# A row factor taken out of two norms and put behind the projections, in a two-block transformer kernel on one core

## The chip, the core and the metric

The program runs on one core of one Trainium2 chip, in fp32 data with fp32r matmuls. [...] The metric is the device time of one execution in microseconds.

## The reference

Two blocks follow each other on x of 512 tokens by 1024 columns. Both begin with the same norm and then project its result many times:

```
def rmsnorm(x, g):
    r = lax.rsqrt(jnp.mean(xf * xf, axis=-1, keepdims=True) + EPS)   # one factor per token (row)
    return (xf * r) * g                                              # g: one gain per column

# block 1
h = rmsnorm(x, norm1_g); u, v_a, q, k, v_b = split(h @ w_in)
y_a = chunked_spatial_gating(u, rmsnorm(v_a, ...), w_s, b_s)          # u * z
y_b = rmsnorm(diff_attention(rmsnorm(q), rmsnorm(k), v_b))
gates = sigmoid(h @ w_gate + b_gate)
x = x + (g_a * (y_a @ w_up_a) + g_b * (y_b @ w_up_b)) @ w_out
x = x + hierarchical_moe(rmsnorm(x, norm2_g))                         # 32 experts, top 2
# block 2
xn = _rms(x, norm_gain); proj = xn @ w_in
qkv_a = silu(causal_dwconv(proj[:, :1536], conv_w))                   # 4 taps along the tokens
o_a = gated_delta_rule(l2n(q_a), l2n(k_a), v_a, g, beta);  o_b = stick_breaking(_rms(q_b), _rms(k_b), v_b)
out = x + (gate_a * ((_rms(o_a) * silu(z_a)) @ w_up_a) + gate_b * ((o_b * silu(z_b)) @ w_up_b)) @ w_out
```

r is a scalar per token, so (r·x·g) W = r · ((x·g) W): the factor can be applied ahead of a projection or behind it. In block 2 it has to be applied ahead of the convolution, which mixes tokens.

## The kernel before

Every projection is a call of `dense`: 512 tokens by 512 columns, 1024 deep. SP loads the raw weights in two transfers of 1 MB (raw_q_0 and raw_q_4 for the projection q), ACT casts each quarter (two of the eight 128-row slabs) to a high part in wHL (L58, CAST), and DVE, or POOL for the quarters that `pool_split` names, subtracts to get the low part (L59). For each of eight slabs d and each of four accumulators acc_0 to acc_3 three matmuls of 128x512 are done: high by high, high by low, low by high. `stationary="x"` leaves tokens on the partitions of the accumulator (L89 to L91), `stationary="w"` leaves columns there and tokens along the free side (L93 to L95). The four accumulators come from one pool of four, so the next projection's acc_t can be written only when the evacuation of acc_t, `evac(t)`, has read it; wHL has two buffers and raw two.

The activations are split the same way. `row_rms` squares x on ACT (in block 1 the second half of x on DVE), adds, and finds r by a chain of thirteen small DVE operations (L130, and L40 to L47 in `rsqrt_newton`). `transpose_x` then multiplies all of x by r (L105, eight operations into the tiles xn_h1 or xn_h3), does 32 PE transposes into eight PSUM tiles psT, and splits each into hH (ACT, L52, scaled by the column gain) and hL (DVE, L53). Each slab d of the first projection needs hH and hL of d.

The first projection of block 1 is q (acc_q), then k, v and the rest; of block 2 ak, aq and av (acc_ak, acc_aq, acc_av), which `delta_inputs` evacuates with three convolution taps on DVE (L1025), a copy U and a scaled copy cv on ACT (L1022, L1023), a tanh, and four transposes (psck, pscq, pscv); then qbA, qbB and so on. Ahead of block 2 stands the mixture of experts, whose `combine` adds each pair's result (psc, L854 and L855) to x on DVE (L856). Accumulators psc and acc share a pool.

The order on each engine is set by the tile scheduler from the order of the code, its priorities and the buffers. `issue_after` ties one instruction behind another.

Of the kernel before, what the change touches and what calls it, by code (L numbers as in the profile page):

```python
# [73 lines left out]
def dense(K, xs, W, n0, nk, evac, name, stationary="x", width=512, hook=None):  # L74
# [3 lines left out]
    for k in range(0, nk, 2):  # L78
        wHL = K.wp.tile([P, 2, 2, width], R, name=f"wHL_{name}_{k}", tag="wHL", bufs=K.nwh)
        wH, wL = wHL[:, 0], wHL[:, 1]  # L80
        split_plain(K, wH, wL, raws[k // 4][:, k % 4:k % 4 + 2], nc.gpsimd if k // 2 in K.pool_split else None)
        for kk in range(2):
            d = k + kk
            H, L = xs(d)
            for t in range(4):
                ts = slice(t * P, t * P + P)
                s, e = d == 0, d == nk - 1
                if stationary == "x":
                    nc.tensor.matmul(acc[t][:, :width], H[:, ts], wH[:, kk], start=s, stop=False)  # L89
                    nc.tensor.matmul(acc[t][:, :width], H[:, ts], wL[:, kk], start=False, stop=False)  # L90
                    nc.tensor.matmul(acc[t][:, :width], L[:, ts], wH[:, kk], start=False, stop=e)  # L91
# [117 lines left out]
def first_attention(K, I, hs, filler):  # L209
# [3 lines left out]
    def load_half(hh):  # L213
        tok = {}
        ssq = {}
        for nm, n0 in (("q", 2048), ("k", 3072)):
# [154 lines left out]
def gating(K, I, hs, Vs):  # L371
# [636 lines left out]
def delta_inputs(K, I, hs, W):  # L1008
# [3 lines left out]
    for ti, nm in enumerate(("k", "q", "v")):  # L1012
# [5 lines left out]
        def ev(h, acc, nm=nm, U=U, T=T, col0=col0, ti=ti):  # L1018
# [567 lines left out]
```

## Time and profile before

| what | value |
|---|---|
| median of 3 runs | 1450.3 us (1449.73 to 1450.57) |
| profiled execution | 1450.06 us, of it the span that the trace shows 1448.2 us |
| busy share of the span | PE 95%, DVE 55%, ACT 35%, POOL 6% |
| mean granted clock of TensorE | 0.988 |

A row of the busy table gives, for each engine, the microseconds in which it had an instruction under way and the number of instructions. A row of the timeline gives the start, the time to the end of a run of like instructions, the engine and line, the output and inputs, and in brackets how long the engine had been idle ahead of it and which instruction ended that. A matmul's row lasts from its start to its modelled end and overlaps the next; the distance between starts is the pace.

### The profile page before, as it was taken

What the parts mean: (1) busy time and instruction counts of PE and PEld (TensorE: products, weight loads), DVE (VectorE), ACT (ScalarE), POOL (GpSimd) and SP (SyncE); (2) the same over time, 40 slices, a digit from 0 to 9 for tenths busy, and PEclk for the clock granted to TensorE, in tenths of its full rate; (3) what the DMA queues carried; (4) which work ended last, traced back from release to release, by engine and by line L of the source; (5) the groups of instructions that cost most, each with busy time, mean ns of one, the idle gap of its engine ahead of it and who ended that gap; (6) DMA issues with size and microseconds to landing.
All of it is one profiled execution on the core that took longest, in us unless ns stands there. A gap on an engine that the chain in (4) does not pass through costs nothing.

```text
span 1448.2 us, 18248 instructions
## 1 busy us (share of the span) xinstructions
PE 1371.1 (95%) x7211; PEld 1015.3 (70%) x7211; DVE 795.7 (55%) x1560; ACT 509.2 (35%) x896; POOL 84.0 (6%) x93
## 2 busy tenths in 40 slices
PE   4999999999999997899999997989999999999998
PEld 3777786788888886344444445769889977667886
DVE  5466578683343255455555447587454656563562
ACT  3435436433223231122111214446332237663331
POOL 2000000000000022100000001110000100001000
PEclk9999999999999998899999998999999999999999
DMA  4221221122232478799999832213220000002332
GB/s 152 91 87 31 89 80 64 43 75 88 89 105 98 131 265 301 293 380 369 365 362 364 320 117 88 87 45 103 87 87 2 31 30 29 30 30 67 137 116 88
DMA packets 73756, 196.12 MB, mean 135 GB/s; under 512 B 8658, under 2 KB 10820, under 8 KB 69572
## 3 DMA queue, kind: packets, MB, share of 16 engines
q1 hardware_dynamic: 67460, 184.79, 35.6%
q0 software_dynamic: 3680, 9.44, 1.9%
q8 instruction: 58, 0.95, 0.3%
q10 hardware_dynamic: 2528, 0.69, 0.2%
q14 instruction: 30, 0.25, 0.0%
HBM read 192.81 MB, written 6.29 MB: 137 GB/s over the span
## 4 chain that ended last, share of the span: by engine, by line
PE 83%; DVE 10%; ACT 4%; issue 1%; DMA 1%; POOL 0%; SPq 0%; DVEq 0%; ACTq 0%
PE acc_e L795 8%; PE po L795 4%; PE acc_upbg L93 3%; PE acc_upbg L95 3%; PE acc_upbg L94 3%; PE acc_gbg L95 2%; PE acc_gbg L93 2%; PE acc_gbg L94 2%; PE pss L270 2%; PE psc L854 2%; PE acc_o L89 2%; PE acc_o L90 2%; PE acc_o L91 2%; PE psc L855 1%; PE psG L786 1%
## 5 line engine op out<-in xcount | busy, mean ns | idle before, releaser
L795 PE MATMUL acc_e<-w,S 128*64 128x512 f32 x512 | 121.0, 604 | 0.0
L856 DVE TENSOR_TENSOR x<-x,psc 128x512 f32<-128x512 f32 x128 | 80.3, 680 | 13.5 <-PE psc L855 13.5
L795 PEld LDWEIGHTS acc_e<-w,S 128*64 128x64 f32 x512 | 41.6, 138 | 55.7 <-issue 52.3
L795 PE MATMUL po<-w,th 128*64 128x512 f32 x256 | 58.5, 598 | 8.1 <-DVE th L819 8.1
L59 DVE TENSOR_TENSOR wHL_upbg<-raw_upbg,wHL_upbg 128x1024 fp32r<-128x1024 f32 x24 | 29.3, 1224 | 55.6 <-ACT wHL_upbg L58 55.6
L59 DVE TENSOR_TENSOR wHL_gbg<-raw_gbg,wHL_gbg 128x1024 fp32r<-128x1024 f32 x20 | 24.5, 1224 | 62.3 <-ACT wHL_gbg L58 62.3
L854 PE MATMUL psc<-Y,DT 128*128 128x512 f32 x128 | 57.8, 451 | 0.3
L855 PE MATMUL psc<-Y,DT 128*128 128x512 f32 x128 | 50.6, 395 | 0.0
L91 PE MATMUL acc_o<-wHL_o,mL_bg 128*128 128x512 f32 x128 | 49.9, 390 | 0.0
L90 PE MATMUL acc_o<-wHL_o,mH_bg 128*128 128x512 f32 x128 | 49.8, 389 | 0.0
L95 PE MATMUL acc_gbg<-hH,wHL_gbg 128*128 128x512 f32 x128 | 49.8, 389 | 0.0
L94 PE MATMUL acc_gbg<-hL,wHL_gbg 128*128 128x512 f32 x128 | 49.8, 389 | 0.0
L58 ACT CAST wHL_upbg<-raw_upbg 128x1024 fp32r<-128x1024 f32 x24 | 25.3, 1053 | 69.7 <-PE acc_upbg L95 47.9
L93 PE MATMUL acc_gbg<-hH,wHL_gbg 128*128 128x512 f32 x128 | 49.5, 389 | 0.0
L89 PE MATMUL acc_o<-wHL_o,mH_bg 128*128 128x512 f32 x128 | 49.2, 391 | 0.0
L837 ACT CAST DT<-psD 128x512 fp32r<-128x512 bf16 x16 | 9.4, 587 | 112.0 <-PE psD L834 112.0
L58 ACT CAST wHL_gbg<-raw_gbg 128x1024 fp32r<-128x1024 f32 x20 | 21.1, 1054 | 73.9 <-PE acc_gbg L95 40.5
L795 PEld LDWEIGHTS po<-w,th 128*64 128x64 f32 x256 | 17.4, 136 | 41.9 <-issue 27.0
L59 DVE TENSOR_TENSOR wHL_o<-raw_o,wHL_o 128x1024 fp32r<-128x1024 f32 x16 | 21.3, 1328 | 45.6 <-ACT wHL_o L58 45.6
L854 PEld LDWEIGHTS psc<-Y,DT 128*128 128x128 f32 x128 | 24.1, 188 | 30.8 <-DVE Y L53 12.2
L52 ACT ACTIVATE Y<-po,cslot 128x512 fp32r<-128x512 f32 x32 | 22.0, 688 | 64.0 <-PE po L795 64.0
L787 DVE COPY S<-psG 128x512 f32<-128x512 f32 x16 | 11.1, 692 | 54.5 <-PE psG L786 52.6
(649 smaller groups left out, 3693.7 us busy)
## 6 DMA issues: line engine op xcount, KB each, us to landing
w<-in_w SPq DMA_DIRECT2D x128, 512.0 KB
w<-in_w SPq DMA_DIRECT2D x32, 1024.0 KB
raw_gbg<-in_w_gate SPq DMA_DIRECT2D x8, 1024.0 KB
raw_o<-in_w_out SPq DMA_DIRECT2D x8, 1024.0 KB
raw_upbg<-in_w_up_a SPq DMA_DIRECT2D x6, 1024.0 KB
raw_upbg<-in_w_up_b SPq DMA_DIRECT2D x6, 1024.0 KB
raw_gr<-in_w_in SPq DMA_DIRECT2D x6, 1024.0 KB
raw_q<-in_w_in SPq DMA_DIRECT2D x4, 1024.0 KB
```

Source lines behind the costliest of these rows:

```text
L58: K.last_h = K.nc.scalar.copy(H, src)
L59: return (eng or K.nc.vector).tensor_sub(L, src, H.bitcast(F))
L89: nc.tensor.matmul(acc[t][:, :width], H[:, ts], wH[:, kk], start=s, stop=False)
L90: nc.tensor.matmul(acc[t][:, :width], H[:, ts], wL[:, kk], start=False, stop=False)
L91: nc.tensor.matmul(acc[t][:, :width], L[:, ts], wH[:, kk], start=False, stop=e)
L93: nc.tensor.matmul(acc[t], wH[:, kk, ts], H, start=s, stop=False)
L94: nc.tensor.matmul(acc[t], wH[:, kk, ts], L, start=False, stop=False)
L95: nc.tensor.matmul(acc[t], wL[:, kk, ts], H, start=False, stop=e)
L795: K.mm_last = K.nc.tensor.matmul(out[js], lhsT[:, js], rhs(j), start=start, stop=stop, tile_position=(0, 64 * j))
L854: nc.tensor.matmul(acc, DT[:, t * P:t * P + P], H[:, n], start=True, stop=False)
L855: nc.tensor.matmul(acc, DT[:, t * P:t * P + P], L[:, n], start=False, stop=True)
L856: nc.vector.tensor_add(out[n][:, t], x[n][:, t], acc)
```

## The change

Four things change together. (1) The squares and r are no longer ahead of the transposes: raw x is transposed and split, in two halves of four slabs. The second half is tied behind the first projection's 48th matmul (`second(last)` at k == 4), and the squares and r behind that. Every fourth transposed tile takes another PSUM buffer ("ob"). (2) r is multiplied in the evacuations of all projections that used the normed x. Where tokens are on the partitions, the copy takes r as its scale (ACT) or a scalar multiply is used (DVE). Where tokens are along the free side, `scale_row` spreads r over the partitions with four matmuls, ACT copies it into the tile alibi, and DVE multiplies the accumulator by that tile; this adds a DVE pass to the gates, to z of the gating, to the delta inputs (there in place of an ACT copy) and to za and zb, and moves half the copies of gr from ACT to DVE. (3) The first loads alternate: half of x, half of q's weights, half of x, half of q's weights. (4) `pool_split` is empty for q and ak, so DVE does those two quarters each; the last expert pair's `combine` goes through the first 512 columns of all four token tiles first; and the stores of x2 follow the second half's splits.

```diff
-def dense(K, xs, W, n0, nk, evac, name, stationary="x", width=512, hook=None):
+def dense(K, xs, W, n0, nk, evac, name, stationary="x", width=512, hook=None, second=None):
     for k in range(0, nk, 2):
+        if k == 4 and second is not None:
+            second(last)
...
-                    nc.tensor.matmul(acc[t], wL[:, kk, ts], H, start=False, stop=e)
+                    last = nc.tensor.matmul(acc[t], wL[:, kk, ts], H, start=False, stop=e)
...
-def transpose_x(K, x, rcol, gcol, hs, name):
-    src = [K.t8.tile([P, 4, 512], F, name=f"xn_{name}{n}", tag="t8") for n in range(2)]
-    for half in range(2):
-        for t in range(4):
-            nc.vector.tensor_scalar_mul(src[half][:, t], x[half][:, t], rcol[:, t:t + 1])
+def transpose_x(K, x, gcol, hs, name, half, last=None):
+    with K.tc.issue_after(last.ins) if last is not None else nullcontext():
+        for d in range(4 * half, 4 * half + 4):
+            tag, bufs = ("ob", 1) if d % 4 == 3 else ("b", 3)
+                nc.tensor.transpose(ps[:, t * P:t * P + P], x[half][:, t, (d % 4) * P:(d % 4) * P + P], K.ident)
+            done = split_scaled(K, H, L, ps, gcol[:, d:d + 1])
...
+def scale_row(K, r, name):
+    ps = K.psb.tile([P, 512], F, name=f"psrow_{name}", tag="b", bufs=3)
+    for t in range(4):
+        K.nc.tensor.matmul(ps[:, t * P:t * P + P], r[:, t:t + 1].to_broadcast((P, P)), K.ident, start=True, stop=True)
+    K.nc.scalar.copy(K.alibi, ps)
+    return K.alibi
...   # q and k; v, va, qbA, qbB, kb and vb likewise
-                nc.scalar.copy(T[:, t], acc)
+                nc.scalar.activation(T[:, t], acc, AF.Copy, scale=K.r1[:, t:t + 1])
-                nc.scalar.activation(junk, acc, AF.Square)
+                nc.scalar.activation(junk, T[:, t], AF.Square)
...   # gating
+            nc.vector.tensor_mul(z[:, gg], z[:, gg], K.rrow)
...   # gate units
+        nc.vector.tensor_mul(g[:, t], acc, K.rrow)
-            nc.scalar.activation(g[:, t], acc, AF.Tanh, bias=..., scale=0.5)
+            nc.scalar.activation(g[:, t], g[:, t], AF.Tanh, bias=..., scale=0.5)
...   # first_block
+    def second(last):
+        done = transpose_x(K, xs, K.cc("g1", 0, 8), hs, "h1", 1, last)
+        with prio(K, K.tc.cur_priority + 60), K.tc.issue_after(done.ins), K.tc.issue_after(K.act_split.ins):
+            row_rms(K, xs, K.r1, "n1", True)
...   # combine, last pair
-    for t in ts:
-        for n in range(2):
+    for n, t in ([(n, t) for t in ts for n in range(2)] if out is x else [(n, t) for n in range(2) for t in ts]):
...   # delta_inputs
-            nc.scalar.activation(y, acc, AF.Copy, scale=K.cc("cw", 36 + j0))
-            nc.scalar.copy(U[:, h, 3:515], acc)
+            nc.vector.tensor_mul(U[:, h, 3:515], acc, K.rrow)
+            nc.scalar.activation(y, U[:, h, 3:515], AF.Copy, scale=K.cc("cw", 36 + j0))
-        K.pool_split = (0, 1) if nm == "k" else (1, 3)
+        K.pool_split = () if nm == "k" else (1, 3)
...   # za, zb
-            K.tanh_last = nc.scalar.activation(th, acc, AF.Tanh, scale=0.5)
-            nc.vector.scalar_tensor_tensor(z[:, t], th, 1.0, acc, op0=OP.add, op1=OP.mult)
+            nc.vector.tensor_mul(z[:, t], acc, K.rrow)
+            K.tanh_last = nc.scalar.activation(th, z[:, t], AF.Tanh, scale=0.5)
+            nc.vector.scalar_tensor_tensor(z[:, t], th, 1.0, z[:, t], op0=OP.add, op1=OP.mult)
```

How the order of instructions moves is shown at three places; numbers behind a name tell buffers apart, and x2 or x4 at a row's end is a count.

PE at the start of the program, where q is the first projection; before:

```order
L109 MATMUL psT_h1_0_155<-ident_87,xn_h10_145 128x128 x2
...
L109 MATMUL psT_h1_2_169<-ident_87,xn_h10_145 128x128 x4
L89 MATMUL acc_q0_0_217<-wHL_q0_0_221,hH0_141 128x512
L90 MATMUL acc_q0_0_217<-wHL_q0_0_221,hH0_141 128x512
L109 MATMUL psT_h1_3_176<-ident_87,xn_h10_145 128x128 x4
L91 MATMUL acc_q0_0_217<-wHL_q0_0_221,hL0_142 128x512
L109 MATMUL psT_h1_4_183<-ident_87,xn_h11_146 128x128 x4
```

and of the change, from the first transposes to the second half's (rows of dots stand for rows left out, here matmuls of the first four slabs):

```order
L109 MATMUL psT_h1_0_114<-ident_91,x0_81 128x128 x4
L109 MATMUL psT_h1_1_121<-ident_91,x0_81 128x128 x4
L109 MATMUL psT_h1_2_128<-ident_91,x0_81 128x128 x4
L109 MATMUL psT_h1_3_135<-ident_91,x0_81 128x128 x4
L91 MATMUL acc_q0_0_145<-wHL_q0_0_149,hH0_110 128x512
L91 MATMUL acc_q0_1_146<-wHL_q0_0_149,hH0_110 128x512
L91 MATMUL acc_q0_2_147<-wHL_q0_0_149,hH0_110 128x512
...
L93 MATMUL acc_q0_3_148<-wHL_q0_2_176,hL0_111 128x512
L109 MATMUL psT_h1_4_203<-ident_91,x1_86 128x128 x4
L109 MATMUL psT_h1_5_210<-ident_91,x1_86 128x128 x4
```

The transposes read x itself, and the 20 that stood among the first matmuls are gone: 16 stand ahead of the first matmul, and 16 behind the 48th.

PE where the experts end and block 2 begins (psc15 is the last pair's combine, acc_ak the first projection of block 2); before:

```order
L855 MATMUL psc1530_6665<-Y15_6610,DT15_6571 128x512
L854 MATMUL psc1531_6669<-Y15_6610,DT15_6571 128x512
L855 MATMUL psc1531_6669<-Y15_6610,DT15_6571 128x512
L109 MATMUL psT_h3_0_6726<-ident_87,xn_h30_6716 128x128 x2
L109 MATMUL psT_h3_1_6733<-ident_87,xn_h30_6716 128x128
...
L109 MATMUL psT_h3_2_6740<-ident_87,xn_h30_6716 128x128 x4
L93 MATMUL acc_ak_0_6790<-h3H0_6712,wHL_ak_0_6794 128x512
L93 MATMUL acc_ak_1_6791<-h3H0_6712,wHL_ak_0_6794 128x512
L109 MATMUL psT_h3_3_6747<-ident_87,xn_h30_6716 128x128 x4
L94 MATMUL acc_ak_0_6790<-h3L0_6713,wHL_ak_0_6794 128x512
```

and of the change:

```order
L877 MATMUL psc1501_6677<-Y15_6630,DT15_6591 128x512
L878 MATMUL psc1501_6677<-Y15_6630,DT15_6591 128x512
L109 MATMUL psT_h3_0_6706<-ident_91,x2_0_6659 128x128
L109 MATMUL psT_h3_1_6713<-ident_91,x2_0_6659 128x128
L877 MATMUL psc1511_6681<-Y15_6630,DT15_6591 128x512
...
L877 MATMUL psc1531_6689<-Y15_6630,DT15_6591 128x512
L878 MATMUL psc1531_6689<-Y15_6630,DT15_6591 128x512
...
L109 MATMUL psT_h3_2_6720<-ident_91,x2_0_6659 128x128 x4
L109 MATMUL psT_h3_3_6727<-ident_91,x2_0_6659 128x128 x4
L95 MATMUL acc_ak_0_6744<-h3H0_6702,wHL_ak_0_6748 128x512
L96 MATMUL acc_ak_0_6744<-h3L0_6703,wHL_ak_0_6748 128x512
```

The last pair's matmuls for the first 512 columns come first, and transposes of those columns (x2_0) stand between those for the other 512.

DVE between the projections ak and aq; before:

```order
L59 TENSOR_TENSOR wHL_ak_4_6848<-raw_ak_4_6788,wHL_ak_4_6848 128x1024
L59 TENSOR_TENSOR wHL_ak_6_6875<-raw_ak_4_6788,wHL_ak_6_6875 128x1024
L59 TENSOR_TENSOR wHL_aq_0_6981<-raw_aq_0_6973,wHL_aq_0_6981 128x1024
L1025 SCALAR_TENSOR_TENSOR cvk0_6902<-Uk_6783,ccols_b_346,cvk0_6902 128x512 x2
L1025 SCALAR_TENSOR_TENSOR cvk1_6919<-Uk_6783,ccols_b_346,cvk1_6919 128x512
L1025 SCALAR_TENSOR_TENSOR cvk0_6902<-Uk_6783,ccols_b_346,cvk0_6902 128x512
L1025 SCALAR_TENSOR_TENSOR cvk1_6919<-Uk_6783,ccols_b_346,cvk1_6919 128x512
L1027 SCALAR_TENSOR_TENSOR cvk0_6902<-cthk0_6903,cvk0_6902 128x512
L1025 SCALAR_TENSOR_TENSOR cvk1_6919<-Uk_6783,ccols_b_346,cvk1_6919 128x512
L1037 TENSOR_REDUCE ssqk_6782<-cthk0_6903 128x4
```

and of the change:

```order
L46 TENSOR_TENSOR rt_n3_6843<-rt_n3_6843,rv_n3_6841 128x4
L47 SCALAR_TENSOR_TENSOR r3_6734<-rt_n3_6843,ry_n3_6842 128x4
L1045 TENSOR_TENSOR Uk_6737<-acc_ak_0_6744,alibi_105 128x512
L1045 TENSOR_TENSOR Uk_6737<-acc_ak_1_6745,alibi_105 128x512
...
L1048 SCALAR_TENSOR_TENSOR cvk0_6918<-Uk_6737,ccols_b_336,cvk0_6918 128x512
L1048 SCALAR_TENSOR_TENSOR cvk1_6935<-Uk_6737,ccols_b_336,cvk1_6935 128x512
...
L1048 SCALAR_TENSOR_TENSOR cvk1_6935<-Uk_6737,ccols_b_336,cvk1_6935 128x512
L1045 TENSOR_TENSOR Uk_6737<-acc_ak_3_6747,alibi_105 128x512
L1050 SCALAR_TENSOR_TENSOR cvk0_6918<-cthk0_6919,cvk0_6918 128x512
L1050 SCALAR_TENSOR_TENSOR cvk1_6935<-cthk1_6936,cvk1_6935 128x512
L1060 TENSOR_REDUCE ssqk_6736<-cthk0_6919 128x4
```

The multiplies from acc_ak, which need r3 and its spread in alibi, stand ahead of the taps, and the one of acc_ak_3 behind six of them. On PE 27 matmuls that write acc_aq_0, 1 and 2 now stand ahead of the first that writes acc_aq_3; before, 24 that write acc_aq_0 and 1 stood ahead of the first that writes acc_aq_2.

## Rows read from the trace of the kernel before

**Rows 1.** The page, part 1, and two of its groups: line, engine, operation, count | busy, mean ns.

```profile
PE 1371.1 (95%) x7211; PEld 1015.3 (70%) x7211; DVE 795.7 (55%) x1560; ACT 509.2 (35%) x896; POOL 84.0 (6%) x93
...
L856 DVE TENSOR_TENSOR x<-x,psc 128x512 f32<-128x512 f32 x128 | 80.3, 680 | 13.5 <-PE psc L855 13.5
...
L59 DVE TENSOR_TENSOR wHL_upbg<-raw_upbg,wHL_upbg 128x1024 fp32r<-128x1024 f32 x24 | 29.3, 1224 | 55.6 <-ACT wHL_upbg L58 55.6
```

**Rows 2.** Busy time by stage: stretch, its length, each engine's busy time, granted clock.

```profile
0.00:45.20 45.20, 26.37 (x121) 21.65 (x122) 22.77 (x52) 14.77 (x23) 7.40 (x13) 1.00 0.46 145
45.20:263.00 217.80, 214.43 (x1071) 165.65 (x1070) 142.36 (x365) 100.63 (x219) 1.61 (x2) 1.00 0.22 73
...
877.60:914.10 36.50, 27.73 (x129) 22.94 (x130) 19.50 (x33) 13.55 (x21) 4.63 (x2) 0.86 0.34 116
914.10:985.00 70.90, 61.58 (x307) 49.72 (x306) 55.10 (x85) 37.81 (x63) 10.47 (x7) 0.98 0.17 53
985.00:1160.00 175.00, 174.39 (x1281) 154.50 (x1281) 94.68 (x181) 56.88 (x104) 9.78 (x22) 1.00 0.20 64
```

**Rows 3.** The timeline of the start, three engines: start, duration, operation, idle before.

```profile
4.70 0.63 ACT L128 ACTIVATE junk_n<-x 128x512 f32<-128x512 f32 x1 [1.70 <-DMA x<-in_x]
...
13.13 1.99 ACT L58 CAST wHL_q<-raw_q 128x1024 fp32r<-128x1024 f32 x2 [5.45 <-DMA crows_b<-in_k_norm_g]
...
14.46 2.20 DVE L47 SCALAR_TENSOR_TENSOR r<-rt_n,ry_n 128x4 f32<-128x4 f32 x1
16.70 5.29 DVE L105 TENSOR_SCALAR xn_h<-x,r 128x512 f32<-128x512 f32 x8
...
19.27 3.01 PE L109 MATMUL psT_h<-ident,xn_h 128*128 128x128 f32 x12 [14.29 <-DVE xn_h L105]
21.93 0.78 PE L89 MATMUL acc_q<-wHL_q,hH 128*128 128x512 f32 x1
...
26.84 0.39 PE L90 MATMUL acc_q<-wHL_q,hH 128*128 128x512 f32 x1
...
29.82 0.39 PE L91 MATMUL acc_q<-wHL_q,hL 128*128 128x512 f32 x1
```

**Rows 4.** The timeline around the second block's first norm, VectorE and TensorE.

```profile
869.66 7.85 DVE L856 TENSOR_TENSOR x<-x,psc 128x512 f32<-128x512 f32 x13
...
879.97 2.34 DVE L46 TENSOR_TENSOR rt_n<-rt_n,rv_n 128x4 f32<-128x4 f32 x1
...
885.82 3.26 DVE L105 TENSOR_SCALAR xn_h<-x,r 128x512 f32<-128x512 f32 x8
...
886.37 3.00 PE L109 MATMUL psT_h<-ident,xn_h 128*128 128x128 f32 x12 [10.46 <-DVE xn_h L105]
889.02 1.20 PE L93 MATMUL acc_ak<-h3H,wHL_ak 128*128 128x512 f32 x2
```

**Rows 5.** TensorE's waits from 877 to 990 us: who waited for whom, total, times, longest.

```profile
PE acc_qbA L90 <- DVE wHL_qbA L59: 2.7, 1, 2.7
...
PE psck L1030 <- DVE cvk L1027: 2.0, 2, 1.5
...
PE acc_aq L95 <- POOL wHL_aq L59: 0.5, 1, 0.5
```

**Rows 6.** Busy time of two stretches at the lower clock.

```profile
880.40:890.60 10.20, 4.23 (x17) 3.50 (x18) 9.92 (x19) 2.37 (x4) 4.19 (x2) 0.50 0.62 214
...
972.50:976.00 3.50, 2.92 (x13) 2.92 (x14) 2.40 (x4) 0.58 (x2) 0.00 (x0) 0.51 0.49 137
```

**Rows 7.** Groups by shape, ScalarE, 0 to 263 us.

```profile
L52 ACT ACTIVATE hH<-psT_h,ccols_a 128x512 fp32r<-128x512 f32 x8 | 5.4, 688 | 7.0 <-PE psT_h L109 7.0
...
L221 ACT COPY qtok<-acc_q 128x512 f32<-128x512 f32 x8 | 4.8, 598 | 5.6 <-PE acc_q L91 5.6
```

**Rows 8.** Groups by shape, VectorE, 877.6 to 1448.2 us.

```profile
L1025 DVE SCALAR_TENSOR_TENSOR cvk<-Uk,ccols_b,cvk 128x512 f32<-128x512 f32 x12 | 10.8, 926 | 2.7 <-ACT Uk L1023 2.6
...
L1025 DVE SCALAR_TENSOR_TENSOR cvv<-Uv,ccols_b,cvv 128x512 f32<-128x512 f32 x12 | 8.6, 746 | 0.4 <-ACT Uv L1023 0.4
```

More of the change, by code (lines that the diff above doesn't have):

```diff
@@ L51, in split_scaled @@
 def split_scaled(K, H, L, src, gain):
-    K.nc.scalar.activation(H, src, AF.Copy, scale=gain)
+    K.act_split = K.nc.scalar.activation(H, src, AF.Copy, scale=gain)
     return K.nc.vector.scalar_tensor_tensor(L, src, gain, H.bitcast(F), op0=OP.mult, op1=OP.subtract)
@@ L59, in split_plain, with load_w @@
     return (eng or K.nc.vector).tensor_sub(L, src, H.bitcast(F))
-def load_w(K, W, n0, width, nk, name, hook=None):
-    parts = []
-    for q in range(0, nk, 4):
+def load_w(K, W, n0, width, nk, name, hook=None, qs=None):
+    parts = K.ahead.pop(name, [])
+    for q in range(4 * len(parts), nk, 4) if qs is None else qs:
         raw = K.wp.tile([P, 4, width], F, name=f"raw_{name}_{q}", tag="raw", bufs=K.nraw)
@@ L90, in dense @@
                     nc.tensor.matmul(acc[t][:, :width], H[:, ts], wL[:, kk], start=False, stop=False)
-                    nc.tensor.matmul(acc[t][:, :width], L[:, ts], wH[:, kk], start=False, stop=e)
+                    last = nc.tensor.matmul(acc[t][:, :width], L[:, ts], wH[:, kk], start=False, stop=e)
                 else:
@@ L451, in first_block @@
     xr = I["x"][0].rearrange("(t p) d -> p t d", p=P)
+    K.ahead["q0"] = []
     for half in range(2):
@@ L456, in first_block @@
         xs.append(t)
+        K.ahead["q0"] += load_w(K, I["w_in"][0], 2048, 512, 8, "q0h", qs=(4 * half,))
     consts_early(K, I)
     K.alibi = alibi(K)
-    r = K.sm.tile([P, 4], F, name="r1")
-    row_rms(K, xs, r, "n1", True)
     h = []
@@ L465, in first_block @@
     hs = sel(h)
-    transpose_x(K, xs, r, K.cc("g1", 0, 8), hs, "h1")
+    transpose_x(K, xs, K.cc("g1", 0, 8), hs, "h1", 0)
+    K.r1 = K.sm.tile([P, 4], F, name="r1")
+    def second(last):
+        done = transpose_x(K, xs, K.cc("g1", 0, 8), hs, "h1", 1, last)
+        with prio(K, K.tc.cur_priority + 60), K.tc.issue_after(done.ins), K.tc.issue_after(K.act_split.ins):
+            row_rms(K, xs, K.r1, "n1", True)
+    K.second = second
     yb, Vs = first_attention(K, I, hs, lambda: gate_values(K, I, hs))
+    K.rrow = scale_row(K, K.r1, "n1")
     consts2(K)
@@ L1360, in second_block @@
     W = I["w_in_2"][0]
-    r3 = K.sm.tile([P, 4], F, name="r3")
-    row_rms(K, x2, r3, "n3", big=K.t8.tile([P, 4, 512], F, name="sqjunk", tag="t8"))
-    K.h_after = K.sq_last
-    for n in range(2):
-        nc.sync.dma_start(x2d.rearrange("(t p) d -> p t d", p=P)[:, :, 512 * n:512 * n + 512], x2[n])
     h = []
@@ L1370, in second_block, with second @@
     hs = sel(h)
-    transpose_x(K, x2, r3, K.cc("g3", 0, 8), hs, "h3")
+    transpose_x(K, x2, K.cc("g3", 0, 8), hs, "h3", 0)
+    r3 = K.sm.tile([P, 4], F, name="r3")
+    sqjunk = K.t8.tile([P, 4, 512], F, name="sqjunk", tag="t8")
+    def second(last):
+        done = transpose_x(K, x2, K.cc("g3", 0, 8), hs, "h3", 1, last)
+        with prio(K, K.tc.cur_priority + 60), K.tc.issue_after(done.ins), K.tc.issue_after(K.act_split.ins):
+            row_rms(K, x2, r3, "n3", big=sqjunk)
+            K.rrow = scale_row(K, r3, "n3")
+            for n in range(2):
+                nc.sync.dma_start(x2d.rearrange("(t p) d -> p t d", p=P)[:, :, 512 * n:512 * n + 512], x2[n])
+    K.second = second
     tok, r = delta_inputs(K, I, hs, W)
@@ L1421, in ev @@
         def ev(t, acc):
-            if t % 2:
-                nc.scalar.copy(Z[:, t], acc)
-            else:
-                nc.vector.tensor_copy(Z[:, t], acc)
+            nc.vector.tensor_mul(Z[:, t], acc, K.rrow)
         dense(K, hs, W, n0, 8, ev, nm, stationary="w")
@@ L1516, in body @@
     K.act_mark = K.load_after = K.h_after = None
+    K.ahead = {}
     K.pool_split = ()
```

42 lines of the change are left out of this document (22 added, 20 removed).

## The prediction

> **What bounds the kernel now.** I read the page's busy table first, then busy time by stage, TensorE's waits, and the timelines where it waits. PE is busy 95% of the span, DVE 55%, ACT 35% [rows 1]. So only PE's idle time can be won, and added work on DVE or ACT costs only where PE waits for it. The stages show where: from 45.2 to 263 us PE is busy 214.43 of 217.80 us, and from 985 to 1160 us 174.39 of 175; but in the first 45.20 us only 26.37, from 877.6 to 914.1 us 27.73 of 36.50, and from 914.1 to 985 us 61.58 of 70.90 [rows 2]. The first two of these poor stretches are the two norms that the change takes apart. The third is the delta inputs, to which it adds work.
>
> At the start PE does nothing useful until 19.27 us: its wait of 14.29 us ends on xn_h, the multiply by r [rows 3]. x was there far earlier, since ACT squares its first tile at 4.70. Between lie the squares, r's chain (its last step, usually some 0.16 us, took 2.20 beside POOL's weight split) and eight multiplies of 5.29 us from 16.70 [rows 3]. The same picture stands at block 2: DVE's additions to x run 869.66 + 7.85 = 877.51, and the first transpose comes at 886.37 after 10.46 us of idle PE [rows 4].
>
> **Term A, the start.** Before, the first q matmul stands at 21.93 and q ends at the stage's end, 45.20. After, the transposes need only x's first half. It has landed by about 6.2 us (an estimate: its first part by 4.70, the second one 0.5 MB transfer later). Sixteen transposes at 3.01/12 = 0.25 us each [rows 3] make 4 us when they wait for nothing: about 9.4 with the hand-over to PSUM, and hH of the fourth slab about 10.3, a split being 0.69 us [rows 7]. The weights' first half now comes third in line, about 9.5. Its cast, 1.99/2 = 1.0 us [rows 3], stands behind the four hH on ACT: first matmul at 11.35. From there: 96 matmuls at (29.82 − 26.84)/13 = 0.23 us [rows 3], 21.8 us; 16 warm transposes at an estimated 0.1 (under half the cold price, since they overlap matmuls), 1.6; the first ten or so at the lower clock, twice the price, 1.9; and 0.6 in the middle, where hH4 stands behind a cast on ACT and PE reaches the fifth slab first. Together 25.9, so q ends near 37.2 instead of 45.2: −8.0. r is ready at about 36.4 (four squares on each of ACT and DVE behind the second splits, r's chain, one weight split of 1.22 us [rows 1] in it), so q's evacuations nearly wait for it; k's first matmul may lose 0.2 more. **A = −7.8**, bounds −5 (weights late by 2 us, and r by 1) and −10 (no extra cold time, no stall in the middle).
>
> **Term B, block 2.** The last pair's first 512 columns are done first. Of the 13 additions, 7.85/13 = 0.60 us each [rows 4], the last four then belong to the second half: x's first half is complete at 877.51 − 4 × 0.60 = 875.1. Its transposes mix with the last combine matmuls; hH of the slabs ends at about 876.5, 877.5, 878.5 and 879.2; the cast of ak's weights follows on ACT, so acc_ak starts at about 880.3, not 889.02 [rows 4]. The low parts on DVE wait for the additions and end at 881.8 with the weights' own. Before, ak took 914.1 − 889.02 = 25.1 us with 20 transposes among its matmuls and its first ones at the lower clock [rows 2, 4]; after, 24.0 with 16 transposes and the same clock. ak ends at 904.3 instead of 914.1: **B = −9.8**, bounds −7.5 and −10.5. The lower bound is a stall of 2 us: r3 is ready only at about 904.8, since eight squares, r's chain and a weight split stand behind the second splits.
>
> The clock is the open point of B. It fell to 0.50 from 880.40 to 890.60, after PE had stood still since 886.37 − 10.46 = 875.91 [rows 4], and PE was busy only 4.23 us in that stretch [rows 6]. After, PE stands still from about 877.4 to 880.3, a third as long. If the clock is then full, B gains another 1 us; I keep it low for the first matmuls. [...]
>
> **Term C, the delta inputs.** Three projections, each evacuated in four steps. Removed: ACT's copy U. Added: one DVE multiply per step from PSUM, 12 at 0.60 to 0.68 us by the addition of the same form [rows 1, 4], 7.7 us, beside 55.10 us of DVE work in a stage of 70.90 [rows 2]. So DVE's load there is under the stage's length; what counts is the order. ACT's scaled copy now waits for U and reads SBUF. A new wait: U needs the spread r3, which is four small matmuls at the end of ak, then an ACT copy that stands behind a cast: the first U ends about 2.3 us after ak. The taps, everything behind them on DVE, and acc_aq_0 wait for it. Before, PE waits here 2.0 us for psck and 0.5 for a POOL split [rows 5], part of which the new wait replaces: ak to aq +1.0. Between aq and av the spread is there, and only the longer chain counts: +0.5. Behind av, DVE has r's chain for q and k, the multiplies of tok2, now three U, then the taps, and only then the low part of qbA's second quarter, which before ended a wait of 2.7 us [rows 5]. Four multiplies more ahead of it, at 0.64: +2.5. **C = +4.0.** Bounds: 0, where the U multiplies fill DVE's gaps and the ACT copies that go free the casts; +6, where each of three boundaries costs 2.
>
> Whether POOL's splits slow U matters by about 1. Beside POOL the taps took 926 ns, without it 746 [rows 8]; if U were slowed alike, it would add 0.18 × 4 per boundary, 0.7. [...] I leave U unslowed.
>
> **Term D, everything else.** ACT's copies with a scale take 688 ns for 598 [rows 7], some 44 of them; the gates, za, zb and gr get DVE passes of 0.68, gating eight more; `scale_row` twice four small matmuls. All stand in stages where PE is busy 98 to 99.6% with DVE at 65 and 54% [rows 2]; the first three accumulators of a projection are free before the next needs them. Only the last can show: **D = +0.7**, bounds 0 and +2. The splits that move from POOL to DVE, four at 1.22 [rows 1], are in A and B, where they also take away the 2.20 and 2.34 us steps of r's chain [rows 3, 4].
>
> Sum: −7.8 − 9.8 + 4.0 + 0.7 = −12.9. From the profiled execution of 1450.06 that is 1437.2; the median of before is 0.24 higher, so 1437.4.
>
> **Rivals.**
> 1. The boundaries cost nothing (C and D at 0, or less where ACT's freed copies help): −17.6, 1432.6, and with A at its far bound 1430.5. For it: DVE's wide margin. Against it: the waits there already end on DVE [rows 5].
> 2. The gain is half as large: A at −5, B at −7.5, C at +6: −6.5 or, with D at 2, −4.5, 1443.8 to 1445.8. For it: r comes just in time at both places, and around the wait behind av the clock fell to 0.51 as well, over 3.5 us [rows 6]; a longer wait there costs again. [...]
> 3. Slower: DVE becomes the bound of the delta section. acc_3 of each projection is free only behind three U and six taps, about 2.3 + 2.0 + 5.6 + 0.7 = 10.6 us after the projection's end. If PE stood still all that time less the 2 us of before, three boundaries would cost 25.8; with A + B at −17.6 that is 8.2 over, 1458.5. It decides from 5.9 us a boundary on. Against it: 27 matmuls, 6.2 us, stand ahead of the first that writes acc_aq_3, so at most 4.4 are bare, and this with the late r3 only.
>
> **How the numbers follow.** My case 0.62, own range 1434 to 1441; rival 1 0.17; rival 2 0.15; rival 3 0.04; 0.02 for a gain eaten by something else, within the bound. A measurement of this kernel tells about 0.2%, 2.9 us, from no change. Rivals 1 and 2 and my case are faster by more than that: 0.94; same 0.02; slower 0.04. The range takes rival 1 and most of 2: 1429.5 to 1445.5.
>
> **What would show it.** After: first acc_q matmul near 11.4 us and k's near 37.5; first acc_ak about 8.7 us earlier against the last combine matmul; PE's waits for xn_h gone; new waits of acc_aq on Uk of about 2 us; DVE's wHL_qbA wait longer than 2.7. It is wrong if x's second half or the weights arrive late (A), if r's chain ends well after q or ak (waits of k and aq for the evacuations over 2 us), or if the clock is low in more of the delta section than before.

## The result

The changed kernel takes 1435.93 us (median of 4 runs, 1431.44 to 1440.17) where the kernel before takes 1450.43: a ratio of 0.9893, 95% interval 0.988 to 0.9906. The forecast was 1437.4, from 1429.5 to 1445.5, and faster. The profiled execution is the longest of the four, 1440.17 us, against 1450.06 before: −9.9 us, of which the span shows −9.8. The medians below leave out two executions that took far longer than all others of their kernels, one of e8 (4692.77 us) and one of e10 (2703.21 us).

The page after, its head and the busy times of TensorE (PE; PEld is its weight loads), VectorE (DVE), ScalarE (ACT) and GpSimd (POOL) [rows 1]; SP is SyncE:

```profile
span 1438.4 us, 18334 instructions
...
PE 1382.1 (96%) x7227; PEld 1026.7 (71%) x7227; DVE 811.8 (56%) x1602; ACT 506.3 (35%) x880; POOL 77.6 (5%) x89
```

PE is busy 11 us longer than before although it does only 16 instructions more; nearly all of that is time at the lower clock, worked out below under e0 (19.8 us lost here, 8.3 before). The timeline of the start after, PE, ACT and DVE, which answers to [rows 3]:

```profile
6.14 3.25 PE L109 MATMUL psT_h<-ident,x 128*128 128x128 f32 x14 [0.66 <-DMA x<-in_x]
...
10.01 1.98 ACT L58 CAST wHL_q<-raw_q0h 128x1024 fp32r<-128x1024 f32 x2
...
11.10 1.20 PE L91 MATMUL acc_q<-wHL_q,hH 128*128 128x512 f32 x4 [1.71 <-ACT wHL_q L58]
...
37.16 0.16 DVE L47 SCALAR_TENSOR_TENSOR r<-rt_n,ry_n 128x4 f32<-128x4 f32 x1
...
37.42 1.27 ACT L234 ACTIVATE qtok<-acc_q,r 128x512 f32<-128x512 f32 x2 [2.80 <-DVE r L47]
...
38.16 0.50 PE L91 MATMUL acc_k<-wHL_k,hH 128*128 128x512 f32 x1 [0.87 <-ACT qtok L234]
```

The wait for xn_h is gone. Transposes run as x lands, and the first q matmul stands at 11.10 us instead of 21.93; its wait of 1.71 us ends on the cast of its weights. r's last step starts at 37.16; ACT, idle for 2.80 us until then, starts q's evacuation behind it, and k's first matmul waits 0.87 us for that evacuation. k starts at 38.16.

The timeline at block 2 and behind ak, which answers to [rows 4]:

```profile
861.90 7.85 DVE L879 TENSOR_TENSOR x<-x,psc 128x512 f32<-128x512 f32 x13
...
870.91 2.01 ACT L58 CAST wHL_ak<-raw_ak 128x1024 fp32r<-128x1024 f32 x2
...
868.08 0.40 PE L878 MATMUL psc<-Y,DT 128*128 128x512 f32 x1
...
872.02 0.50 PE L95 MATMUL acc_ak<-h3H,wHL_ak 128*128 128x512 f32 x1 [2.46 <-ACT wHL_ak L58]
...
899.15 0.58 ACT L123 COPY alibi<-psrow_n 128x512 f32<-128x512 f32 x1
...
899.76 1.89 DVE L1045 TENSOR_TENSOR Uk<-acc_ak,alibi 128x512 f32<-128x512 f32 x3 [3.05 <-ACT alibi L123]
...
900.50 0.50 PE L95 MATMUL acc_aq<-h3H,wHL_aq 128*128 128x512 f32 x1 [1.45 <-DVE Uk L1045]
...
910.56 6.17 DVE L1048 SCALAR_TENSOR_TENSOR cvk<-Uk,ccols_b,cvk 128x512 f32<-128x512 f32 x6
916.66 1.21 DVE L59 TENSOR_TENSOR wHL_aq<-raw_aq,wHL_aq 128x1024 fp32r<-128x1024 f32 x1
...
917.93 1.65 PE L97 MATMUL acc_aq<-h3H,wHL_aq 128*128 128x512 f32 x3 [3.51 <-DVE wHL_aq L59]
```

From the last combine matmul to the first of ak it was 889.02 − 875.51 = 13.5 us; it is 872.02 − 868.08 = 3.9, and 2.46 of that is the wait for the cast, which stands behind four hH. Then comes the price: U waits for alibi, acc_aq for U, and at 917.93 PE has waited 3.51 us for the low part of aq's third quarter, which DVE did behind six taps. PE's waits of the whole run [rows 5] after:

```profile
PE acc_aq L97 <- DVE wHL_aq L59: 3.5, 1, 3.5
...
PE acc_qbA L92 <- DVE wHL_qbA L59: 2.8, 1, 2.8
PE acc_qbA L91 <- DVE Uv L1045: 2.5, 1, 2.5
PE acc_ak L95 <- ACT wHL_ak L58: 2.5, 1, 2.5
PE acc_av L95 <- DVE Uq L1045: 1.8, 1, 1.8
...
PE acc_aq L95 <- DVE Uk L1045: 1.5, 1, 1.5
```

The six taps ahead of that split took 6.17 us in the row above. The six taps before them took 4.05 us; beside the slower six POOL was doing a weight split, from 913.83 to 916.19 us. The waits for psck and pscq have gone, and waits on U and on weight splits have come. By stage [rows 2]:

```profile
0.00:45.20 45.20, 36.80 (x157) 29.28 (x158) 24.74 (x66) 19.90 (x33) 2.73 (x11) 0.96 0.47 147
...
872.00:898.00 26.00, 25.84 (x113) 20.92 (x113) 10.94 (x23) 11.16 (x24) 0.00 (x0) 0.93 0.32 108
898.00:978.20 80.20, 67.83 (x345) 57.24 (x344) 62.97 (x101) 36.81 (x59) 12.04 (x7) 0.94 0.18 54
```

The stretch to 45.2 us has 36.80 us of PE work in it for 26.37. From ak's end to the first matmul of qbB, 898.00 to 978.20, it is now 80.2 us; before it was 988.62 − 914.10 = 74.5. Two landmarks of the kernel before, the first matmuls of k and of qbB:

```profile
47.08 0.47 PE L89 MATMUL acc_k<-wHL_k,hH 128*128 128x512 f32 x1
...
988.62 0.28 PE L89 MATMUL acc_qbB<-wHL_qbB,h3H 128*128 128x260 f32 x1
```

### The profile page after: what moved, and what is told of

Read it like the earlier page. It is cut to its first block, busy times and chain, and to the rows that moved or that the text cites. A ratio compares the mean times of both kernels' runs of the same rounds, so it can differ in the third digit from the quotient of the medians.

```text
span 1438.4 us, 18334 instructions
## 1 busy us (share of the span) xinstructions
PE 1382.1 (96%) x7227; PEld 1026.7 (71%) x7227; DVE 811.8 (56%) x1602; ACT 506.3 (35%) x880; POOL 77.6 (5%) x89
## 5 line engine op out<-in xcount | busy, mean ns | idle before, releaser
L879 DVE TENSOR_TENSOR x<-x,psc 128x512 f32<-128x512 f32 x128 | 80.3, 682 | 13.5 <-PE psc L878 13.5
L59 DVE TENSOR_TENSOR wHL_gbg<-raw_gbg,wHL_gbg 128x1024 fp32r<-128x1024 f32 x20 | 24.5, 1225 | 63.1 <-ACT wHL_gbg L58 63.1
L59 DVE TENSOR_TENSOR wHL_upbg<-raw_upbg,wHL_upbg 128x1024 fp32r<-128x1024 f32 x24 | 29.3, 1224 | 52.6 <-ACT wHL_upbg L58 52.6
L810 DVE COPY S<-psG 128x512 f32<-128x512 f32 x16 | 11.1, 692 | 54.4 <-PE psG L809 52.6
```

Source lines behind the costliest of these rows:

```text
L59: return (eng or K.nc.vector).tensor_sub(L, src, H.bitcast(F))
L879: nc.vector.tensor_add(out[n][:, t], x[n][:, t], acc)
```

## The experiments

Each kernel was timed beside the kernel before on the same chip, and each ratio is to that and isn't quite the quotient of the two medians. The groups of kernels ran on different chips. "Delta stage" is the profile's time from the first matmul of ak to the first of qbB, and "PE idle" is that time less PE's busy time in it.

| kernel | median us | ratio to before, interval | delta stage us | PE idle in it us |
|---|---|---|---|---|
| before | 1450.4 to 1452.5 | 1 | 99.6 | 9.3 |
| changed | 1435.93 | 0.9893 (0.988 to 0.9906) | 106.2 | 12.5 |
| e0, changed again | 1432.71 | 0.9865 (0.9849 to 0.988) | 106.2 | 12.5 |
| e1, block 1 only | 1440.53 | 0.9919 (0.9905 to 0.9932) | 101.4 | 7.7 |
| e2, block 2 only | 1446.02 | 0.9965 (0.9952 to 0.9979) | 106.1 | 12.5 |
| e3, no U multiply | 1429.25 | 0.9849 (0.9834 to 0.9864) | 100.7 | 9.2 |
| e4, early r | 1430.49 | 0.9866 (0.9839 to 0.9894) | 102.0 | 9.7 |
| e6, x first | 1434.16 | 0.9869 (0.9849 to 0.9889) | 106.2 | 12.7 |
| e7, U copied by ACT | 1426.46 | 0.9822 (0.9799 to 0.9845) | 101.1 | 9.1 |
| e8, e4 and e7 | 1427.33 | 0.9831 (0.981 to 0.9853) | 101.5 | 10.6 |
| e9, combine by tokens | 1433.72 | 0.9891 (0.9865 to 0.9917) | 101.9 | 11.2 |
| e10, e7 and early casts | 1422.86 | 0.9797 (0.9784 to 0.9809) | 102.5 | 10.9 |
| e11, e7 without POOL | 1423.06 | 0.9792 (0.9775 to 0.9809) | 93.7 | 2.9 |
| e12, all three | 1424.58 | 0.9819 (0.9805 to 0.9832) | 92.2 | 2.9 |

**e0, the spread.** No edit. 

> The changed kernel once more, to see how far its time and its granted clock move from run to run, since four runs lay between 1431 and 1440 us. Theory (the spread is the clock): the runs lie on a line of time against mean granted clock, about 1.1 us for each 0.001, and the stretches at the lower clock differ from the profile shown. Rival (the spread is something else, such as DMA): runs of one clock differ by over 3 us.

Busy time and granted clock (the third figure from a row's end) in the same stretches, the changed kernel's first profile:

```profile
530.00:536.00 6.00, 6.00 (x26) 5.00 (x26) 0.47 (x1) 0.28 (x1) 0.00 (x0) 0.72 0.90 302
...
916.00:926.00 10.00, 8.07 (x27) 6.57 (x28) 4.45 (x6) 3.11 (x6) 0.30 (x2) 0.66 0.33 107
1240.00:1246.00 6.00, 6.00 (x23) 4.57 (x22) 3.54 (x7) 5.05 (x11) 0.00 (x0) 0.72 0.01 1
1268.00:1276.00 8.00, 8.00 (x25) 6.08 (x26) 3.38 (x6) 6.12 (x12) 0.00 (x0) 0.57 0.00 0
```

and e0, profiled at 1433.96 us:

```profile
530.00:536.00 6.00, 6.00 (x21) 4.85 (x20) 0.00 (x0) 0.00 (x0) 0.00 (x0) 0.73 0.98 344
...
914.00:924.00 10.00, 7.68 (x25) 6.29 (x26) 4.85 (x6) 2.80 (x5) 0.69 (x2) 0.66 0.32 107
1240.00:1246.00 6.00, 6.00 (x36) 5.30 (x35) 5.12 (x10) 4.44 (x10) 0.00 (x0) 1.00 0.00 1
1268.00:1276.00 8.00, 7.90 (x38) 5.21 (x37) 6.80 (x12) 5.71 (x12) 0.00 (x0) 1.00 0.00 0
```

The first profile has the lower clock at 1240 and 1268 us, where PE is busy all the time, and e0 has not. Counting each stretch as (1 − clock) times PE's busy time, 19.8 us are lost in the first profile and 12.8 in e0; that is 7.0 apart, and their times are 6.2 apart. The eight runs of the two sets lie near one line as well, from 1440.17 us at a mean clock of 0.981 to 1431.44 at 0.989, none more than 1.3 us off it. The theory holds: the kernel's two sets, 1435.93 and 1432.71, are one kernel with more or less of the lower clock. From here, differences of medians under some 4 us are read with the profile, or between runs of the same mean clock.

**e1 and e2, one block each.** e1 keeps block 2 of before (one of its gates is multiplied by block 1's r besides); e2 keeps block 1 of before (one gate of block 2 lacks r).

> Only block 1 has the change; block 2, its first norm, its delta inputs and the last combine are those of before. Theory: q starts near 11.1 and k near 38.2 us as in the changed kernel, and the time is 8 to 10.5 us under before (the span to the gates 10.5, less what the clock takes back). Rival (the two blocks' gains hang together by the clock): under 6 us.

> Only block 2 has the change; block 1 is that of before. Theory: ak ends 8.3 us earlier against the experts' end, the delta inputs give 5.7 back, of it 2.4 to 3.4 by the clock: 1 to 6 us under before. Rival (the delta inputs give back only 4.0 as predicted and B is 9.8): 6 us or more under before.

The first ak matmul of e1, where the old norm stands, and of e2:

```profile
878.67 1.20 PE L95 MATMUL acc_ak<-h3H,wHL_ak 128*128 128x512 f32 x2
```

```profile
880.38 0.50 PE L95 MATMUL acc_ak<-h3H,wHL_ak 128*128 128x512 f32 x1 [2.46 <-ACT wHL_ak L58]
```

Against their last combine matmuls, at 865.14 and 876.43, these are 13.5 and 4.0 us. Block 1 gives 11.1 us, block 2 5.6; together 16.7, near e0's 18.9. e1 gains a little more than its theory's 10.5, and most of the gain is block 1's. e2's 5.6 lies inside its theory's 1 to 6, but its interval, 3.0 to 7.0 us, reaches over the rival's 6. Its profile is the theory's: ak ends 8.6 us earlier against the last combine matmul, and from ak's end to qbB it is 5.6 us longer than before.

**e3 and e7, what costs in the delta inputs.** e3 leaves r out of the convolution's input:

```diff
-            nc.vector.tensor_mul(U[:, h, 3:515], acc, K.rrow)
-            nc.scalar.activation(y, U[:, h, 3:515], AF.Copy, scale=K.cc("cw", 36 + j0))
+            nc.scalar.activation(y, acc, AF.Copy, scale=K.cc("cw", 36 + j0))
+            nc.scalar.copy(U[:, h, 3:515], acc)
```

> The changed kernel with the delta inputs' U and first tap copied by ACT from the accumulator as before, so that r is left out of the delta inputs' convolution. Theory (the DVE multiply, its wait for the spread r, and what stands behind it cost the delta stage): 4 to 7 us faster than the changed kernel, acc_aq no longer waits for Uk, and qbA starts earlier. Rival (the stage is longer because of the low clock and of POOL's splits, whoever makes U): within 2 us of the changed kernel.

e7 keeps the multiply, behind a copy:

```diff
-            nc.vector.tensor_mul(U[:, h, 3:515], acc, K.rrow)
+            nc.scalar.copy(U[:, h, 3:515], acc)
+            nc.vector.tensor_mul(U[:, h, 3:515], U[:, h, 3:515], K.rrow)
```

> The changed kernel, but ACT first copies the accumulator into U as before, and DVE multiplies U by r in place, so the accumulators come free without r. DVE's work is the same. Theory (what costs in the delta inputs is that accumulators wait for r and for DVE): the waits of acc_aq, acc_av and acc_qbA on U, 1.5, 1.8 and 2.5 us, go: 3 to 6 us faster than the changed kernel. Rival (DVE's added 7.7 us itself is the cost): the waits move to the weight splits, and it is within 1.5 us.

PE's waits of e7 from 860 to 990 us:

```profile
PE pscq L1054 <- DVE cvq L1051: 3.7, 2, 2.2
PE pscv L1054 <- DVE cvv L1051: 2.8, 1, 2.8
PE acc_ak L95 <- ACT wHL_ak L58: 2.5, 1, 2.5
PE psck L1054 <- DVE cvk L1051: 2.3, 2, 1.8
```

The delta stages of before, e0, e7 and, for later, e11, with PE's busy time behind the length:

```profile
889.02:988.62 99.60, 90.28 (x455) 74.02 (x453) 66.18 (x101) 49.07 (x80) 10.47 (x7) 0.97 0.18 54
...
870.42:976.58 106.16, 93.62 (x456) 78.18 (x457) 73.93 (x124) 47.99 (x83) 12.06 (x7) 0.94 0.22 67
...
867.72:968.77 101.05, 91.94 (x457) 76.77 (x457) 76.46 (x122) 54.66 (x95) 10.59 (x7) 0.95 0.23 70
...
870.95:964.66 93.71, 90.80 (x457) 75.59 (x457) 71.07 (x123) 53.88 (x95) 0.79 (x3) 0.96 0.24 76
```

Without the multiply the delta stage is 5.4 us shorter than e0's, and with the multiply but free accumulators 5.1. Part of that is the clock: the lower clock took 6.5 us of the stage in e0, 3.0 in e3 and 5.1 in e7. PE's idle time leaves the slower matmuls out: it is 9.3 us before, 12.5 in e0, 9.2 in e3 and 9.1 in e7. It too moves between profiles of the same code there (9.3 in before and 7.7 in e1, 12.5 in e0 and 11.2 in e9), but the step from 12.5 to 9.1 is clear of that. So the 3.2 us of waiting that the change added are gone both without the multiply and with a multiply behind a copy. DVE's added work costs nothing that shows; that accumulators wait for r and for DVE's queue is what costs. The waits on U are gone but for 0.2 us behind ACT's copy, and psck, pscq and pscv are back, as before the change. By medians e3 is 3.5 us faster than e0, under its theory's 4 and with overlapping intervals, and e7 6.2, just over its theory's 6. At the same mean clock e3 is 2.3 to 3.2 us faster than the changed kernel and e7 3.0 to 6.6, so both rivals are out, e3's narrowly.

**e4 and e8, r earlier.** `row_rms` stands ahead of the second half's transposes, tied to the second weight cast (in block 1 also to its split).

> The changed kernel, but the squares and r of both blocks follow the first half's splits (at the start behind the second quarter's weight split) instead of the second half's. Theory (r comes just in time at q's end and the spread of r3 late at ak's end): k's waits for qtok, 1.4 us, and aq's first wait for Uk, 1.45 us, go: 2 to 4 us faster than the changed kernel. Rival (the late r is hidden by what else is late at these two places, the weight splits): within 1 us, and the waits come back under another name.

> Early r and U copied by ACT together. Theory: the two add, 5 to 9 us faster than the changed kernel, near 1425. Rival (DVE's load): 2 to 4 us, with the weight splits as the last wait.

e4's ratio, which has two runs at a clock of 0.980 in it, is that of e0. At a clock of 0.987 e4 takes 1429.61 to 1430.10 us and e0 1432.56 and 1432.86: 2.5 to 3.3 us, inside the theory's 2 to 4. But the theory named the wrong waits. k doesn't wait in e4, but it doesn't in e0 either, so its wait of 1.4 us was one of the first profile alone; and aq still waits 1.8 us for Uk. What went is aq's wait of 3.5 us for its third split, for which one of 1.8 us on psck has come, and the delta stage is 4.2 us shorter, 1.3 of it by the clock. e8 is no faster than e7: once accumulators come free without r, early r brings nothing. Its time lies inside the expected 5 to 9 us, but e7 alone gives 6.2, so the two don't add, as e8's theory had it.

**e6 and e9, the load order and the combine order**, each set back to that of before.

> The changed kernel with the loads in the order of before: both halves of x, then q's weights. Theory (the weights' first half decides the first matmul): x1 ahead of it delays it by one 1 MB transfer, some 2.7 us, and the first q matmul comes at 12 to 13.5 instead of 11.1: 1 to 2.5 us slower than the changed kernel. Rival (hH and the cast decide): no difference.

> The changed kernel with the last pair's combine by token tiles as before. Theory (x's first half is complete four additions, 2.4 us, earlier through the new order): acc_ak starts 1 to 2.5 us later against the experts' end, and the time is 1 to 2.5 us longer than the changed kernel's. Rival (the splits' low parts and the weights' cast end last anyway): within 0.7 us.

e6's first q matmul:

```profile
13.60 2.07 PE L91 MATMUL acc_q<-wHL_q,hH 128*128 128x512 f32 x4 [4.21 <-ACT wHL_q L58]
```

It comes 2.5 us later than the changed kernel's, and the wait for the weights' cast is 4.21 us for 1.71. The medians, 1434.16 against 1432.71 on another chip, can't tell it. Runs of the same mean clock can: at 0.989 five runs of e6 take 1433.51 to 1434.50 us and two of the changed kernel 1431.44 and 1431.49, so the old order costs 2.0 to 3.1 us, and that much of block 1's 11.1 is the load order's. In e9 ak starts 4.97 us after the last combine matmul instead of 3.94: 1.0 us, the theory's lower end, and the times don't tell it. e9's waits in the delta stage are those of e0 but for one that is 1.3 us shorter, and yet its stage is 4.3 us shorter: the lower clock took 3.4 us there instead of 6.5.

**e10 to e12, better versions.** e10 lifts the tie that held ak's first casts behind hH, e11 sets `pool_split = ()` for all three delta projections, e12 does both; each has e7's copy.

> U copied by ACT, as in the kernel that was 6 us faster than the changed one, and besides the casts of ak's first weights free to run in ACT's idle time ahead of block 2. Theory (acc_ak's wait of 2.5 us for the cast is the last one at block 2's start): the wait goes, and it is 1.5 to 2.5 us faster than U copied alone, near 1424.5. Rival (hL on DVE, behind the additions, comes as late): under 1 us.

> U copied by ACT, and the delta projections' weight splits all on DVE, none on POOL. Theory (an operation with two SBUF inputs waits for POOL's split as a whole, so each POOL split costs DVE some 2 us and saves it 1.2): the multiplies and taps fall from 1138 and 922 ns to about 0.69, PE's waits for psck and pscq shrink, 1 to 3 us faster than U copied alone. Rival (DVE's four added splits come in the same places): no difference.

> U copied by ACT, the casts of ak's first weights early, and no POOL splits in the delta projections. Theory (three separate waits: accumulators, the cast, POOL's lock): the gains of 6.2, 3.3 and 3.4 us add to 12 to 13 under the changed kernel, near 1420. Rival (they share a cover or the clock takes one back): 1422 to 1424, like the better two.

Mean times of the taps and of the multiply, e0 (U from PSUM):

```profile
L1048 DVE SCALAR_TENSOR_TENSOR cvk<-Uk,ccols_b,cvk 128x512 f32<-128x512 f32 x12 | 10.2, 922 | 0.0
...
L1045 DVE TENSOR_TENSOR Uk<-acc_ak,alibi 128x512 f32<-128x512 f32 x4 | 2.6, 686 | 3.1 <-ACT alibi L123 3.1
```

e7 (U in place, in SBUF, POOL still splitting):

```profile
L1049 DVE SCALAR_TENSOR_TENSOR cvk<-Uk,ccols_b,cvk 128x512 f32<-128x512 f32 x12 | 10.3, 922 | 0.0
...
L1046 DVE TENSOR_TENSOR Uk<-Uk,alibi 128x512 f32<-128x512 f32 x4 | 4.4, 1138 | 3.5 <-ACT alibi L123 3.5
```

e11 (no POOL splits):

```profile
L1049 DVE SCALAR_TENSOR_TENSOR cvk<-Uk,ccols_b,cvk 128x512 f32<-128x512 f32 x12 | 8.1, 747 | 0.0
...
L1046 DVE TENSOR_TENSOR Uk<-Uk,alibi 128x512 f32<-128x512 f32 x4 | 2.6, 686 | 0.0
```

Beside a split on POOL (895.46 to 897.85 us in e7) the multiply in place took 1138 − 686 = 0.45 us more than in e11 on average over four: the first three took 3.71 us together, the fourth, behind the split, 0.68. This is the wait that e12's theory calls POOL's lock. The one from PSUM took 686 ns in e0, with a split on POOL beside it (897.72 to 900.09 us). In e10 the wait for ak's cast is gone, and from the last combine matmul to qbB it takes 103.8 us where e7 takes 105.0. e10 and e11 are 3.6 and 3.4 us under e7 by medians, with intervals that overlap e7's and lie clear of e0's. At a clock of 0.989 e10 is 1.4 to 4.2 us faster than e7, and at 0.986 e11 is 5.4 to 7.9. e11's gain is in its profile: without POOL's splits PE's idle time in the delta stage falls from 9.1 to 2.9 us, by more than the 3.4 of free accumulators. That is far under before's 9.3 too, so the kernel before was probably paying for its splits on POOL as well; no run tests that. No run takes these splits out and leaves the accumulators waiting for r, so what they cost the changed kernel as it stands is open; nor does one give POOL back the splits of q and ak. e12's delta stage is the shortest, and it isn't faster. Two stretches of its profile:

```profile
1126.00:1143.00 17.00, 17.00 (x122) 13.12 (x123) 3.35 (x11) 3.19 (x7) 2.36 (x1) 0.60 0.07 15
1199.00:1207.00 8.00, 8.00 (x25) 6.30 (x26) 4.25 (x8) 5.37 (x12) 0.91 (x1) 0.57 0.40 131
```

PE is busy in all of these 25 us, at a mean clock near 0.6; that is 10.2 us lost, and e11's profile lost 3.4 behind the delta stage (15.2 and 13.2 us in the whole profiles). All five runs of e12 have a clock of 0.983 or 0.984. The rival was right for e12's time. Why the clock falls just there stays open. The best versions shown are e10 and e11, 1423 us, by their ratios 2.0 to 2.1% under before.

## Why the prediction came out

The time was right, but in part by luck, as a sum of errors that offset one another. Its mechanism, transposes that no longer wait for r in both blocks and a price in the delta inputs, is what e1, e2 and the rows show. The profiled pair, from landmark to landmark, against the terms:

- **A, forecast −7.8.** k starts 47.08 − 38.16 = 8.9 us earlier (10.4 in e0). The first q matmul was forecast for 11.35 and came at 11.10, q's end for 37.2 and came at 37.0. The step that failed is the other side: "q ends at the stage's end, 45.20" took the edge of a window for an event; before, k started at 47.08. k's first matmul waited 0.87 us instead of 0.2, and 1.4 in two waits, as r was just late; in e0 it didn't wait at all.
- **B, forecast −9.8.** acc_ak starts 9.6 us earlier against the last combine matmul (forecast 8.7). The failed step is ak's own length, forecast 24.0 and measured 26.0 for 25.1 before: 1.7 us of it went at the lower clock (0.50 from 873 to 876 us), 0.8 before, so leaving four transposes out saves nothing that shows. That ak would start at the same low clock as before was the author's estimate, and no run shows it: before, the clock was 0.50 at ak's first matmuls (889 to 890 us), after 0.97 (872 to 873 us), and it fell behind them. At ak's end the gain is 8.7.
- **C, forecast +4.0.** 80.2 − 74.5 = +5.7, inside its bounds. Of that, 3.4 is the lower clock, which took 4.8 us here and 1.4 before; the sum had no term for it. The failed step is the split: the three boundaries were to lose 1.0, 0.5 and 2.5, and from one landmark to the next (ak's end, first matmuls of av, qbA and qbB) it is +5.8, −0.7 and +0.6. DVE's six taps, slowed beside POOL (6.17 us for 4.05), stood ahead of aq's third split (3.51 us), and the clock fell at the end of that wait (0.50 from 918 to 924 us). And the waits that were added are those of accumulators and of what stands behind U, not DVE's 7.7 us of work (e7).
- **D, forecast +0.7.** From k's start to the start of block 1's last projection (acc_o) another 1.6 us are won, and from qbB to the end 0.6 lost. That loss is the lower clock, 5.1 us of it there for 1.7 before; e0, which has none there, wins 3.9. So D's sign was wrong: multiplies and scaled copies cost nothing that shows, and in block 2's last stage PE's waits went. The change took half of gr's copies off ACT, which would fit; no run tests it. The largest of these waits, before and after:

```profile
PE psob L1337 <- ACT LS L1335: 2.0, 2, 1.5
...
PE psob L1360 <- ACT LS L1358: 0.5, 2, 0.3
```

- **Not in the sum**: +3.1 us between that projection and the last combine, where only the order of the last combine was changed. This is the clock: it was low for 3.4 us from 531 on with PE busy (0.50 from 532 to 535), and longer from 558 to 580, which took 6.4 us for 3.1 before. Profiles without the first of these (e4, e7, e8, e12) take 362.0 to 362.3 us for this stretch, before 361.7, the changed kernel 364.8.

−8.9 − 1.6 + 3.1 − 8.7 + 5.7 + 0.6 = −9.8. In e0 the same landmarks give −10.4 − 1.9 + 3.3 − 8.7 + 5.7 − 3.9 = −15.9, so the forecast of −12.9 lies between two profiles of one kernel that differ by the clock. Two of its sums are a little off, without weight: 96 matmuls at 0.23 us make 22.1 us, not 21.8, and 1450.3 − 17.6 is 1432.7. Of the prediction's signs of being wrong one came: the clock was low in more of the delta section than before.

Rival 1 (the boundaries cost nothing) is what e3 and e7 show once the accumulators are free: from ak's end to qbB they take 74.8 and 75.1 us, before 74.5. Rival 3 (DVE as the bound) needed 5.9 us at every boundary, and the three cost 5.7 together; e7, with no less work on DVE, is faster. Rival 2's clock was real (3.4 of C's 5.7 us), but it isn't tied to waits alone: in e9 the same wait of 3.5 us ahead of aq's third split has the full clock behind it (1.00 from 916 to 926 us). That POOL's splits leave U unslowed was the author's choice between two values, and the runs agree with it: the three U multiplies that ran in the changed kernel beside a split on POOL (899.33 to 901.70 us) took 1.89 us together. Beside POOL's splits the multiply with one input from PSUM stayed at 686 ns (e0), and the one with both in SBUF went to 1138 (e7).

## What to carry to other kernels

Where a norm's row factor is all that holds transposes back, put it behind the projection: here the work it adds was hidden under PE's, and the wait for the factor at PE's start had not been. But an evacuation that needs the factor holds the accumulator; copy the accumulator out first with an engine that needs nothing, and multiply afterwards (PE's idle time in the delta stage fell from 12.5 to 9.1 us in e7). Look too for weight splits on POOL beside DVE operations with two SBUF inputs: taking them off was worth 6.2 us of PE's idle time here (9.1 us in e7, 2.9 in e11). Read the end of a stage from its events, and see what the first instruction behind it does.

## What was not expected of the hardware

The granted clock falls to 0.50 also in stretches where PE has been busy throughout by the trace (whose matmul ends are modelled). In before it does so between 1224 and 1230 us (0.50 from 1226 to 1228), but not at 531:

```profile
530.00:536.00 6.00, 6.00 (x29) 4.85 (x28) 3.44 (x5) 2.51 (x6) 0.76 (x1) 1.00 1.03 410
...
1224.00:1230.00 6.00, 6.00 (x24) 4.76 (x23) 4.70 (x9) 5.83 (x13) 0.12 (x1) 0.72 0.00 0
```

Such falls come at a few places of the program, in some profiles and not in others. One place is 4 us behind the first router logits (pslog), near 531 us, in the changed kernel, e0, e6, e10 and e11 alone. Three more lie behind the first output of block 2's second attention (psob): by 7 to 8 us in before, e4 and e12, by 34 us in the changed kernel, e6 and e9, and by 60 to 62 us in these three and e4, e7 and e11. e12's stretch at 1128 us is in no other profile. Why they come in one profile and not in the next stays open.

Counted as under e0, such a stretch took 1.7 us (at 1225 us in before, at 531 and 1241 in the changed kernel), 3.4 (at 1268 in the changed kernel) or 6.8 (at 1128 in e12). All of the lower clock, also that at starts and behind gaps, took 6.7 to 19.8 us of the profiles of the changed kernel and its variants, and 8.3 of before; of it, stretches with PE busy throughout took nothing in e3 and e8, 6.8 us in the changed kernel's first profile and 10.2 in e12. That is as much as the experiments' differences.
